# Differential attention: two query tiles' scores in one run of matmuls, and projections with two PSUM banks

## The chip, the cores and the metric

The kernel runs on one NeuronCore of a Trainium2 chip. Its metric is the device time of one execution in microseconds. The core's engines work side by side, each through its own list of instructions: TensorE (PE) multiplies into PSUM, which has eight banks of 512 fp32 columns for 128 partitions; VectorE (DVE) and ScalarE (ACT) read the banks and do everything else that is elementwise; SyncE (SP) issues the loads.

## What is computed

Two layers over 256 latent and 256 context tokens of width 1024. A layer normalizes its input, feeds three mixers (a recurrent one, multi-head latent attention, differential attention), adds them through gates, and ends with a feed-forward part. The changed part is differential attention, with 8 heads, two maps of queries and keys of width 64, and one map of values of width 128:

```python
def _attention(q, k, v, mix_w, scale):
    # out = sum_m mix_w[m] * softmax(scale * q_m k_m^T) v
    def block(qi):
        s = jnp.einsum('bqmhd,bkmhd->bmhqk', qi, k).astype(jnp.float32) * scale
        p = jnp.einsum('m,bmhqk->bhqk', w, jax.nn.softmax(s, axis=-1))
        return jnp.einsum('bhqk,bkhd->bqhd', p.astype(v.dtype), v)
...
wc = jnp.stack([jnp.ones((), jnp.float32), -lam])
o_c = _attention(_diff_qk(dq, lp['diff_q_g'], rope_diff), jnp.concatenate([kd_l, kd_c], axis=1),
                 jnp.concatenate([vd_l, vd_c], axis=1), wc, DIFF_SCALE)
...
if need_ctx:      # layer 0 only: context queries read context keys alone
    o_cc = _attention(_diff_qk(dqc, lp['diff_q_g'], None), kd_c, vd_c, wc, DIFF_SCALE)
```

## The kernel before

Every fp32 operand is split into a high and a low part (names ending in H and L), and a product is three matmuls, high by high, low by high and high by low (L200 to L202). Weights are streamed in pieces of 128 x 1024 by SP and split on the way: ScalarE writes the high part (`wh`), VectorE the low part (`wl`; both L138). In layer 1 there are more weight buffers, whose tile is called `room`.

Tokens are worked in tiles of 128. Layer 0 has four query tiles (0 and 1 latent, 2 and 3 context) and layer 1 the two latent ones. Latent queries see 512 keys, context queries 256.

A scheduler places the instructions on the engines by a priority that counts up as the code is written. Work written as a generator stands in a queue, and `fill(ns)` draws from it so many nanoseconds of matmuls, so that projections fill PE between the steps of attention. `PAIR_FIRST` (2000) puts the score matmuls ahead. Each engine then runs its list in order, and a waiting instruction holds up all behind it.

PSUM's banks are given out by pools with tags, each tag in rotation: a tile gets its bank when the last reader of the tile before in that bank is done. Before the change `mm` (L93) has three banks for projections, `tr` two for transposes, and three more are given out anew by stage (`three_banks`, L100): in the stage of differential attention one pair of banks, tag `S2`, for the scores of both maps of one query tile, and one bank `sc` for the product with the values (`po`).

That stage, from 298 to 560 us in layer 0 and 1398 to 1580 us in layer 1, is the loop at L1133. For head i it writes: `diff_prep(i + 1)` (transposes `dtrk` and `dtrq`, split into `dkH`, `dkL`, `dqH`, `dqL`); `probs_T` of head i - 1 (transposes `ptr` of the probabilities, split into `pH` and `pL`); `diff_sc(i)` (scores `S` at L663, softmax with one maximum on VectorE, L621, and one exponential `dp` on ScalarE, L623, for each tile and map, then the difference of the maps, L966); `diff_sub(i - 2)` (`subt2`); and `diff_pv(i - 1)` (`po`, twelve matmuls, copied by ScalarE to `so`, L989, transposed to `subt`, normalized). `diff_proj` makes queries, keys and values of two heads through `gemm_tm` (L449), and `v_tm` splits the values from the projection's bank into `dvH` and `dvL`, tiles of a pool with six buffers (`t_v`). `gemm_tm` loads each of the two halves of a weight once and works it through all token tiles, so that four token tiles hold two banks, `pst0` and `pst1`, from the first half to the second.

At the stage's end, beside the last heads, the queue holds the first projections of the recurrent branch and of the gates: `rnn_conv` (L1021), a convolution of four taps, one operation on ScalarE (L1030) and three on VectorE (L1034) for each projection's bank, which layer 0 first copies out of PSUM to `xr` (L1025) and layer 1 reads in place; and `branch_gate` (L1114), whose bank ScalarE copies to `gt` (L1118).

## Time and profile before

| | us |
|---|---|
| median of three runs (1972.23, 1972.54, 1977.07) | 1972.54 |
| profiled execution | 1974.12 |
| its span | 1972.3 |
| TensorE busy | 1930.2 |
| VectorE busy | 1568.3 |
| ScalarE busy | 1069.9 |

The span runs from the first to the last instruction of the core. Busy time of an engine is the time in which it has an instruction in work; matmuls overlap, so that their durations add up to more than the time they take. In a timeline the difference of two starts is what a matmul costs. The granted clock is the share of TensorE's full speed: 1.0 is 2.4 GHz and 0.5 is 1.2 GHz.

### The profile page before, as it was taken

Reading aid. Unit: us, or ns where it says so; the run is one execution under the profiler, and the core shown is the slowest. Engines: PE = TensorE matmul, PEld = TensorE weight load, DVE = VectorE, ACT = ScalarE, POOL = GpSimd, SP = SyncE. Lnnn points to the kernel's source line nnn. Section 1 sums busy time; section 2 is a strip of 40 time slices with the busy share of each in tenths; the row PEclk is TensorE's granted clock in tenths of the full one; section 3 lists DMA queues with packets and bytes.
Section 4 is the critical chain, followed back from the end, with each engine's and each line's share of the span. In section 5 each row is a group of like instructions: output and inputs, shape, how many; then the busy total and the mean of one; then the engine's idle time right before and its main releaser. Section 6 shows DMA issues by size and latency. Waiting matters only on the chain. (4 is left out here: it accounts for less than half of the span.)

```text
span 1972.3 us, 31832 instructions
## 1 busy us (share of the span) xinstructions
PE 1930.2 (98%) x11746; PEld 1666.3 (84%) x11746; DVE 1568.3 (80%) x3838; ACT 1069.9 (54%) x1975; POOL 58.8 (3%) x198
## 2 busy tenths in 40 slices
PE   7999999999999999999999999999999999899999
PEld 4888888988678878888888888988999788898888
DVE  5679965788798888789888876898688889966763
ACT  4568833455576663353233224798444678845552
POOL 0001000000000000000000000012010000000000
PEclk9999999999999999999999999999999999999999
DMA  8311122212234456536656653422322234474553
GB/s 291 99 41 51 53 65 77 76 55 67 70 102 129 140 191 197 184 127 201 196 191 201 200 176 115 151 64 76 128 93 80 65 123 143 156 231 150 185 189 108
DMA packets 91068, 258.16 MB, mean 131 GB/s; under 512 B 10144, under 2 KB 17312, under 8 KB 90656
## 3 DMA queue, kind: packets, MB, share of 16 engines
q1 hardware_dynamic: 90912, 256.13, 39.8%
q8 instruction: 92, 1.51, 0.3%
q14 instruction: 64, 0.52, 0.1%
HBM read 250.85 MB, written 5.24 MB: 130 GB/s over the span
## 5 line engine op out<-in xcount | busy, mean ns | idle before, releaser
L138 ACT ACTIVATE wh<-st 128x1024 fp32r<-128x1024 f32 (+4 forms) x305 | 308.4, 1012 | 367.8 <-PE ps L201 173.1
L138 DVE TENSOR_TENSOR wl<-st,wh 128x1024 fp32r<-128x1024 f32 (+4 forms) x305 | 354.2, 1162 | 125.5 <-ACT wh L138 122.0
L200 PE MATMUL ps<-hH,wh 128*128 128x512 f32 (+1 forms) x504 | 182.0, 361 | 3.8 <-ACT gt L1118 2.9
L202 PE MATMUL ps<-hH,wl 128*128 128x512 f32 (+1 forms) x504 | 180.6, 359 | 1.7 <-DVE wl L138 1.7
L201 PE MATMUL ps<-hL,wh 128*128 128x512 f32 (+1 forms) x504 | 181.3, 360 | 0.0
L200 PE MATMUL pst<-wh,hH 128*128 128x256 f32 x568 | 164.3, 289 | 0.0
L201 PE MATMUL pst<-wl,hH 128*128 128x256 f32 x568 | 162.1, 285 | 0.0
L202 PE MATMUL pst<-wh,hL 128*128 128x256 f32 x568 | 161.9, 285 | 0.0
L200 PE MATMUL ps<-h2H,wh 128*128 128x512 f32 (+1 forms) x368 | 139.1, 381 | 0.7 <-ACT h2H L379 0.7
L201 PE MATMUL ps<-h2L,wh 128*128 128x512 f32 (+1 forms) x368 | 139.5, 380 | 0.0
L202 PE MATMUL ps<-h2H,wl 128*128 128x512 f32 (+1 forms) x368 | 139.5, 380 | 0.0
L621 DVE TENSOR_REDUCE st<-S 128x1 f32<-128x512 f32 (+1 forms) x192 | 113.0, 596 | 21.4 <-ACT dp L623 11.2
L138 DVE TENSOR_TENSOR room<-acc,room 128x1024 fp32r<-128x1024 f32 (+3 forms) x75 | 87.6, 1169 | 30.6 <-ACT room L138 29.1
L200 PEld LDWEIGHTS pst<-wh,hH 128*128 128x128 f32 x568 | 108.6, 191 | 3.8 <-issue 3.3
L200 PEld LDWEIGHTS ps<-hH,wh 128*128 128x128 f32 x504 | 95.3, 189 | 19.3 <-ACT gt L1118 3.9
L202 PEld LDWEIGHTS pst<-wh,hL 128*128 128x128 f32 x568 | 108.5, 191 | 1.7 <-issue 1.4
L201 PEld LDWEIGHTS pst<-wl,hH 128*128 128x128 f32 x568 | 108.6, 191 | 1.1 <-issue 0.7
L202 PEld LDWEIGHTS ps<-hH,wl 128*128 128x128 f32 x504 | 95.2, 189 | 15.6 <-DVE wl L138 2.3
L310 DVE SCALAR_TENSOR_TENSOR ms<-ms,cb 128x512 f32<-128x512 f32 x160 | 107.3, 688 | 1.3
L138 ACT ACTIVATE room<-acc 128x1024 fp32r<-128x1024 f32 (+3 forms) x75 | 76.2, 1017 | 57.6 <-PE ps L201 20.5
L201 PEld LDWEIGHTS ps<-hL,wh 128*128 128x128 f32 x504 | 95.3, 189 | 12.8
L310 DVE SCALAR_TENSOR_TENSOR sq<-ms,cb 128x512 f32<-128x512 f32 x112 | 75.7, 689 | 31.9 <-DMA ms<-wmodt 31.0
(585 smaller groups left out, 5558.3 us busy)
## 6 DMA issues: line engine op xcount, KB each, us to landing
st<-wfm SPq DMA_DIRECT2D x224, 512.0 KB, 3.5
ms<-wmodt SPq DMA_DIRECT2D x160, 256.0 KB, 2.8
acc<-wfm SPq DMA_DIRECT2D x56, 512.0 KB, 3.5
st<-wfo SPq DMA_DIRECT2D x35, 512.0 KB, 3.5
mstage<-wmod SPq DMA_DIRECT2D x16, 512.0 KB, 5.3
acc<-wfo SPq DMA_DIRECT2D x9, 512.0 KB, 3.5
st<-wlru SPq DMA_DIRECT2D x7, 512.0 KB, 3.4
st<-wukv SPq DMA_DIRECT2D x13, 256.0 KB, 2.6
```

The lines of the kernel that those rows point to most:

```text
L138: return A.activation(dH, src, AF.Copy), V.tensor_tensor(out=dL, in0=src, in1=f(dH), op=ALU.subtract)
L200: nc.tensor.matmul(ps, wH, xH, start=start, stop=False, skip_group_check=skip)
L201: nc.tensor.matmul(ps, wH, xL, start=False, stop=False, skip_group_check=skip)
L202: nc.tensor.matmul(ps, wL, xH, start=False, stop=stop, skip_group_check=skip)
L310: issue_after(V.scalar_tensor_tensor(out=o, in0=st, scalar=1.0, in1=cb[:, v, :], op0=ALU.mult, op1=ALU.mult, accum_out=sums[:, i - i0, h, ...
L621: V.tensor_reduce(out=st[:, 0:1], in_=S, axis=AX.X, op=ALU.max, negate=True)
```

## The change

The three banks of a stage become four, and `mm` keeps two fixed ones. Outside the stage of differential attention the fourth is the third `mm` bank, as before. Inside it the four are two pairs `S2`: projections have two banks, and `po` takes a bank of a pair.

`scores2` now takes two query tiles. For the latent tiles it takes both pairs, one for a tile; for the context tiles, which have 256 keys, one pair, each tile in one half of the columns. The twelve matmuls (two tiles, three products, two maps) are chained one behind the other, where there were two runs of six. The first waits for the last readers of the tiles that were in its banks (`readers`, in which each exponential and each copy of `po` is entered). In layer 1 the run takes its tiles in reverse.

`gemm_tm` works one pair of token tiles through both halves of the weight before the next, so that one bank at a time is filled, and keeps both halves until the end.

```diff
-    def ps_mm(name):
-        return pp.tile([P, 512], F32, tag="mm", name=name, bufs=3)
...
+    def four_banks(stage, two):
 
         if spare[0] is not None:
             spare[0].close()
         spare[0] = ctx.enter_context(ExitStack())
         banks[0] = spare[0].enter_context(tc.tile_pool(name=stage, bufs=1, space=PSUM, reuse_waits="tile"))
-
-    three_banks("sc")
-    singles = [3]
+        pairs[0] = two
+
+    four_banks("sc", False)
+    third = [0]
+
+    def ps_mm(name):
+        third[0] = (third[0] + 1) % 3
+        if third[0] == 0 and not pairs[0]:
+            return banks[0].tile([P, 512], F32, tag="mm", name=name, bufs=1)
+        return pp.tile([P, 512], F32, tag="mm", name=name, bufs=2)
+
+    readers, taken = {}, [0]
+
+    def ps_pair(name):
+        taken[0] += 1
+        return banks[0].tile([P, 2, 512], F32, tag="S2", name=name, bufs=2)
 
     def ps_sc(name):
-        return banks[0].tile([P, 512], F32, tag="sc", name=name, bufs=singles[0])
+        if pairs[0]:
+            return ps_pair(name)[:, 0, :]
+        return banks[0].tile([P, 512], F32, tag="sc", name=name, bufs=3)
...
     def gemm_tm(l, widx, xH, xL, toks, ps_, consume):
 
-        pss = [ps_(f"pst{i}").rearrange("p (t n) -> p t n", t=2) for i in range(len(toks) // 2)]
-        for hf in range(2):
-            H, L = wload(wfm[l, widx, hf])
-            H = H.rearrange("p (k n) -> p k n", n=256)
-            L = L.rearrange("p (k n) -> p k n", n=256)
-            for i, tt in enumerate(toks):
-                for kk in range(4):
-                    k = hf * 4 + kk
-                    mm3(pss[i // 2][:, i % 2, :], xH[:, k, tt * P:(tt + 1) * P], xL[:, k, tt * P:(tt + 1) * P], H[:, kk, :], L[:, kk, :], k == 0 and i % 2 == 0, k == KT - 1 and i % 2 == 1, True)
-                if hf == 1 and i % 2 == 1:
-                    consume(toks[i - 1], pss[i // 2])
-                yield 12 * mm_ns(256)
+        W = []
+        for t0 in toks[::2]:
+            ps = ps_("pst").rearrange("p (t n) -> p t n", t=2)
+            for hf in range(2):
+                if t0 == toks[0]:
+                    W.append([w_.rearrange("p (k n) -> p k n", n=256) for w_ in wload(wfm[l, widx, hf])])
+                H, L = W[hf]
+                for i in range(2):
+                    tok = slice((t0 + i) * P, (t0 + i + 1) * P)
+                    for kk in range(4):
+                        k = hf * 4 + kk
+                        mm3(ps[:, i, :], xH[:, k, tok], xL[:, k, tok], H[:, kk, :], L[:, kk, :], k == 0 and i == 0, k == KT - 1 and i == 1, True)
+                    if hf == 1 and i == 1:
+                        consume(t0, ps)
+                    yield 12 * mm_ns(256)
...
-            def scores2(qH, qL, kH, kL, tt):
-
-                k0 = 0 if tt < 2 else SEQ
+            def scores2(qH, qL, kH, kL, tts):
+
+                ctx_ = tts[0] >= 2
+                k0 = SEQ if ctx_ else 0
                 n = T - k0
-                both = banks[0].tile([P, 2, 512], F32, tag="S2", name="S", bufs=1)
-                S = [both[:, m, :] for m in range(2)]
-                tok = slice(tt * P, (tt + 1) * P)
+                both = [ps_pair("S") for _ in range(1 if ctx_ else 2)]
+                at_ = {tt: taken[0] if ctx_ else taken[0] - 1 + i for i, tt in enumerate(tts)}
+                S = {tt: [both[0][:, m, i * n:(i + 1) * n] if ctx_ else both[i][:, m, :] for m in range(2)] for i, tt in enumerate(tts)}
                 before = None
-                for i, (q_, k_) in enumerate(((qH, kH), (qH, kL), (qL, kH))):
-                    for m in range(2):
-                        K = slice(64 * m, 64 * m + 64)
-                        mm = nc.tensor.matmul(S[m][:, :n], q_[K, tok], k_[K, k0:], start=(i == 0), stop=(i == 2), tile_position=(64 * m, 0))
-                        if before is not None:
-                            issue_after(mm, before)
-                        else:
-                            tc.cur_priority -= PAIR_FIRST
-                        before = mm
+                for at, tt in enumerate(tts[::-1] if last else tts):
+                    tok = slice(tt * P, (tt + 1) * P)
+                    for i, (q_, k_) in enumerate(((qH, kH), (qH, kL), (qL, kH))):
+                        for m in range(2):
+                            K = slice(64 * m, 64 * m + 64)
+                            mm = nc.tensor.matmul(S[tt][m], q_[K, tok], k_[K, k0:], start=(i == 0 and not (ctx_ and at)), stop=(i == 2 and not (ctx_ and at == 0)), tile_position=(64 * m, 0), skip_group_check=ctx_)
+                            if before is not None:
+                                issue_after(mm, before)
+                            else:
+                                for b_ in set(at_.values()):
+                                    if b_ - 2 in readers:
+                                        issue_after(mm, readers[b_ - 2])
+                                tc.cur_priority -= PAIR_FIRST
+                            before = mm
                 tc.cur_priority += PAIR_FIRST
-                return [s_[:, :n] for s_ in S]
+                return S, at_
...
                 for tt in qtoks:
+                    if tt % 2 == 0:
+                        S, at_ = scores2(*qk, (tt, tt + 1))
                     p1 = pc[0][1] if tt == 3 else t_p("dp1")
                     sl = slice(0, 512) if tt < 2 else slice((tt - 2) * 256, (tt - 1) * 256)
                     p2 = t_p("dp2")
                     rr = []
-                    S = scores2(*qk, tt)
                     for m, dst, total in ((0, p1[:, sl], s0[:, tt:tt + 1]), (1, p2[:, sl], None)):
-                        rr.append(softmax_raw(S[m], rq[:, tt, 2 * hh + m:2 * hh + m + 1], dst, total))
+                        rr.append(softmax_raw(S[tt][m], rq[:, tt, 2 * hh + m:2 * hh + m + 1], dst, total))
+                    readers[at_[tt]] = last_exp[0]
                     V.scalar_tensor_tensor(out=rr[1], in0=rr[1], scalar=s0[:, tt:tt + 1], in1=nlam, op0=ALU.mult, op1=ALU.mult)
...
             def diff_pv(h):
                 o = ps_sc("po")
+                at_ = taken[0]
...
-                A.activation(u[:, :TQ], o[:, :TQ], AF.Copy)
+                readers[at_] = A.activation(u[:, :TQ], o[:, :TQ], AF.Copy)
...
-            three_banks(f"pair{l}")
-            singles[0] = 1
+            four_banks(f"pair{l}", True)
+            readers.clear()
...
-            three_banks(f"single{l}")
-            singles[0] = 3
+            four_banks(f"single{l}", False)
```

In the changed kernel the lines of the three matmuls of a product are L212 to L214, that of the scores is L681.

PE at the first scores of head 1 in layer 0 (`S` are scores, `pst` a projection, `dtrk` and `dtrq` transposed keys and queries; x2 stands for the two maps), before:

```order
L201 MATMUL pst1_4515<-wl_4519,hH_145 128x256
L202 MATMUL pst1_4515<-wh_4518,hL_146 128x256
L663 MATMUL S_4606<-dkH_3864,dqH_3873 128x512 x2
L663 MATMUL S_4606<-dkL_3865,dqH_3873 128x512 x2
L663 MATMUL S_4606<-dkH_3864,dqL_3874 128x512 x2
L200 MATMUL pst1_4515<-wh_4518,hH_145 128x256
L201 MATMUL pst1_4515<-wl_4519,hH_145 128x256
```

and in the changed kernel:

```order
L214 MATMUL pst_4513<-wh_4546,hL_146 128x256
L681 MATMUL S_4608<-dkH_3864,dqH_3873 128x512 x2
L681 MATMUL S_4608<-dkL_3865,dqH_3873 128x512 x2
L681 MATMUL S_4608<-dkH_3864,dqL_3874 128x512 x2
L681 MATMUL S_4609<-dkH_3864,dqH_3873 128x512 x2
L681 MATMUL S_4609<-dkL_3865,dqH_3873 128x512 x2
L681 MATMUL S_4609<-dkH_3864,dqL_3874 128x512 x2
L960 MATMUL dtrk_4562<-ident_92,ddk_4421 128x128
L960 MATMUL dtrk_4562<-ident_92,ddk_4427 128x128
```

Where one query tile's run of six stood between projection matmuls, one run has the six of both tiles.

PE behind the product with the values (`po`) of head 0 in layer 0, up to its transposes `subt`; the last `po` matmul stands five rows ahead of the first row here, before:

```order
L201 MATMUL pst0_4868<-wl_4873,hH_145 128x256
L202 MATMUL pst0_4868<-wh_4872,hL_146 128x256
L663 MATMUL S_4704<-dkH_3864,dqH_3873 128x256 x2
L663 MATMUL S_4704<-dkL_3865,dqH_3873 128x256 x2
L663 MATMUL S_4704<-dkH_3864,dqL_3874 128x256 x2
L200 MATMUL pst0_4868<-wh_4872,hH_145 128x256
L201 MATMUL pst0_4868<-wl_4873,hH_145 128x256
L202 MATMUL pst0_4868<-wh_4872,hL_146 128x256
L992 MATMUL subt_4772<-ident_92,so_4770 128x128 x4
L939 MATMUL dtrk_4800<-ident_92,ddk_4447 128x128
```

and in the changed kernel, from the last two `po` matmuls on:

```order
L1010 MATMUL po_4755<-pL_4604,dvH_3905 128x256
L1011 MATMUL po_4755<-pH_4603,dvL_3906 128x256
L1016 MATMUL subt_4770<-ident_92,so_4768 128x128 x4
L960 MATMUL dtrk_4798<-ident_92,ddk_4421 128x128
L960 MATMUL dtrk_4798<-ident_92,ddk_4427 128x128
L960 MATMUL dtrk_4798<-ident_92,ddk_4485 128x128
L960 MATMUL dtrk_4798<-ident_92,ddk_4487 128x128
L212 MATMUL pst_4873<-wh_4876,hH_145 128x256
L213 MATMUL pst_4873<-wl_4877,hH_145 128x256
```

Before, matmuls of the next projection and a run of scores stand between `po` and `subt`; now `subt` follows at once, and the next projection (`pst_4873`) comes behind it.

PE near the end of the stage in layer 1, where the second bank of the convolution's projection ends (`ps1`) and the gate's projection begins (`ps0_17715` before, `ps0_17707` now), before:

```order
L201 MATMUL ps1_17516<-hL_12521,room_12752 128x512
L202 MATMUL ps1_17516<-hH_12520,room_12752 128x512
L200 MATMUL ps0_17715<-hH_12520,wh_17718 128x256
L986 MATMUL po_17569<-pL_17491,dvH_17116 128x256
L987 MATMUL po_17569<-pH_17490,dvL_17117 128x256
L985 MATMUL po_17569<-pH_17490,dvH_17116 128x256
L986 MATMUL po_17569<-pL_17491,dvH_17116 128x256
L987 MATMUL po_17569<-pH_17490,dvL_17117 128x256
L201 MATMUL ps0_17715<-hL_12521,wh_17718 128x256
L202 MATMUL ps0_17715<-hH_12520,wl_17719 128x256
```

and in the changed kernel:

```order
L213 MATMUL ps1_17515<-hL_12513,room_12744 128x512
L214 MATMUL ps1_17515<-hH_12512,room_12744 128x512
L1016 MATMUL subt_17576<-ident_92,so_17574 128x128 x2
L650 MATMUL ptr_17645<-ident_92,dp1_17501 128x128
L650 MATMUL ptr_17645<-ident_92,dp1_17531 128x128
L650 MATMUL ptr_17645<-ident_92,dp1_17501 128x128
L650 MATMUL ptr_17645<-ident_92,dp1_17531 128x128
L1009 MATMUL po_17668<-pH_17650,dvH_17110 128x256
L212 MATMUL ps0_17707<-hH_12512,wh_17710 128x256
L213 MATMUL ps0_17707<-hL_12513,wh_17710 128x256
```

The gate's projection stood right behind the last matmul of `ps1`, in a third bank; now the rest of the attention stands between, and its bank is that of `ps0_17514`, the convolution's other projection.

VectorE in the changed kernel at that place (`room` is a weight's low part, `dp1` the difference of the maps, `subr` and `subrt` small steps of the normalization, `xc` the convolution out of the banks `ps0` and `ps1`):

```order
L150 TENSOR_TENSOR room_12744<-acc_12745,room_12744 128x1024
L640 RECIPROCAL st4_17537<-st4_17537 128x1
L224 SCALAR_TENSOR_TENSOR subrv_17584<-subss_17580,s0_17383 128x2
L988 SCALAR_TENSOR_TENSOR st4_17537<-st4_17537,s0_17486,nlam_10259 128x1
L225 TENSOR_SCALAR subr_17586<-subrv_17584 128x2
L989 SCALAR_TENSOR_TENSOR dp1_17531<-dp2_17532,st4_17537,dp1_17531 128x512
L226 TENSOR_SCALAR subr_17586<-subr_17586 128x2
L1058 SCALAR_TENSOR_TENSOR xc_17615<-ps0_17514,prm1_83,xc_17615 128x2x254
L229 SCALAR_TENSOR_TENSOR subrt_17585<-subr_17586 128x2
L1058 SCALAR_TENSOR_TENSOR xc_17636<-ps1_17515,prm1_83,xc_17636 128x2x254
L230 TENSOR_TENSOR subrt_17585<-subrt_17585,subrv_17584 128x2
L1058 SCALAR_TENSOR_TENSOR xc_17615<-ps0_17514,prm1_83,xc_17615 128x2x255
```

The operations of the two convolutions stand in turns, with the small steps between them; three more follow.

## Rows read from the trace of the kernel before

**Rows 1.** The page, busy time of each engine (share of the span), instructions.

```profile
PE 1930.2 (98%) x11746; PEld 1666.3 (84%) x11746; DVE 1568.3 (80%) x3838; ACT 1069.9 (54%) x1975; POOL 58.8 (3%) x198
```

**Rows 2.** Waits of PE by line: total us, times, longest us.

```profile
PE ps L202 <- DVE room L138: 5.5, 2, 4.1
PE ps L200 <- ACT gt L1118: 2.9, 2, 2.2
...
PE S L663 <- ACT dp L623: 0.6, 2, 0.3
```

**Rows 3.** Timeline of PE around one run of scores: start us, duration us, operation.

```profile
452.59 0.28 PE L202 MATMUL pst<-wh,hL 128*128 128x256 f32 x1
452.80 0.39 PE L663 MATMUL S<-dkH,dqH 64*128 64x256 f32 x2
453.02 0.28 PE L663 MATMUL S<-dkL,dqH 64*128 64x256 f32 x2
453.14 0.28 PE L663 MATMUL S<-dkH,dqL 64*128 64x256 f32 x2
453.35 0.39 PE L200 MATMUL pst<-wh,hH 128*128 128x256 f32 x1
453.57 0.28 PE L201 MATMUL pst<-wl,hH 128*128 128x256 f32 x1
```

**Rows 4.** Instructions on tile S: count, ns min/median/max, first and last start, forms.

```profile
L663 PE MATMUL S<-dkH,dqH x96: 381/493/503, 298.5 to 1564.8; 64*128 64x512 f32 x64, 64*128 64x256 f32 x32
```

**Rows 5.** Timeline of PE in layer 1's tail, with [idle before <- releaser].

```profile
1557.98 0.50 PE L663 MATMUL S<-dkH,dqH 64*128 64x512 f32 x2 [0.30 <-ACT dp L623]
...
1559.38 0.98 PE L635 MATMUL ptr<-ident,dp 128*128 128x128 f32 x7 [0.43 <-DVE dp L966]
...
1566.48 0.30 PE L635 MATMUL ptr<-ident,dp 128*128 128x128 f32 x1 [0.34 <-DVE dp L966]
```

**Rows 6.** Timeline of PE from the last po matmul to subt, layer 0.

```profile
465.58 0.28 PE L987 MATMUL po<-pH,dvL 128*128 128x256 f32 x1
...
466.55 0.66 PE L992 MATMUL subt<-ident,so 128*128 128x128 f32 x4
```

**Rows 7.** Groups of ScalarE by line and form, 290 to 560 us: busy, mean ns | idle.

```profile
L138 ACT ACTIVATE wh<-st 128x1024 fp32r<-128x1024 f32 x33 | 34.9, 1057 | 35.6 <-PE ps L201 24.1 <-PE pst L202 11.3
L623 ACT ACTIVATE dp<-S,st,drq 128x512 f32<-128x512 f32 x32 | 24.9, 777 | 17.0 <-DVE st L622 15.5 <-DVE subrt L218 1.5
...
L138 ACT ACTIVATE pH<-ptr 128x512 fp32r<-128x512 f32 x24 | 14.1, 597 | 12.1 <-PE ptr L638 7.5 <-PE ptr L635 4.6
...
L138 ACT ACTIVATE dvH<-pst 128x256 fp32r<-128x256 f32 x16 | 5.9, 380 | 9.2 <-PE pst L202 4.9 <-DVE dvL L138 2.5 <-PE po L986 1.8
...
L989 ACT ACTIVATE so<-po 128x512 f32<-128x512 f32 x8 | 4.8, 597 | 1.7 <-PE po L987 1.7
```

**Rows 8.** Timeline of VectorE in layer 1's tail.

```profile
1563.99 1.23 DVE L138 TENSOR_TENSOR room<-acc,room 128x1024 fp32r<-128x1024 f32 x1 [0.89 <-ACT room L138]
...
1565.58 0.75 DVE L966 SCALAR_TENSOR_TENSOR dp<-dp,st,dp 128x512 f32<-128x512 f32 x1
1566.25 0.74 DVE L1034 SCALAR_TENSOR_TENSOR xc<-ps,prm,xc 128x508 f32<-128x508 f32 x1
...
1568.30 0.16 DVE L213 TENSOR_SCALAR subr<-subrv 128x2 int32<-128x2 int32 x1
1568.37 0.74 DVE L1034 SCALAR_TENSOR_TENSOR xc<-ps,prm,xc 128x510 f32<-128x510 f32 x1
```

**Rows 9.** Timeline of PE after a wait of layer 1, 1717 to 1720 us.

```profile
1716.89 0.58 PE L202 MATMUL ps<-hH,room 128*128 128x256 f32 x1 [4.14 <-DVE room L138]
...
1719.84 0.32 PE L200 MATMUL ps<-hH,room 128*128 128x256 f32 x1
1719.99 0.28 PE L201 MATMUL ps<-hL,room 128*128 128x256 f32 x1
```

**Rows 10.** One stretch: length, busy us (count) by engine, PEclk, DMA share, GB/s.

```profile
1717.00:1720.00 3.00, 3.00 (x15) 3.00 (x16) 3.00 (x8) 0.11 (x1) 0.00 (x0) 0.51 0.67 196
```

More of the change, by code (lines that the diff above doesn't have):

```diff
@@ L90, in tile_hybrid @@
     pp = ctx.enter_context(tc.tile_pool(name="pp", bufs=1, space=PSUM, reuse_waits="tile"))
-    def ps_mm(name):
-        return pp.tile([P, 512], F32, tag="mm", name=name, bufs=3)
     def ps_tr(name):
         return pp.tile([P, 512], F32, tag="tr", name=name, bufs=2)
-    spare, banks = [None], [None]
-    def three_banks(stage):
+    spare, banks, pairs = [None], [None], [False]
+    def four_banks(stage, two):
         if spare[0] is not None:
@@ L287, in first_mod @@
         V.tensor_scalar(out=am[:, :, t], in0=modt[0][:, 1, :, t], scalar1=1.0, scalar2=prmt[0][:, N1 + t:N1 + t + 1], op0=ALU.add, op1=ALU.mult)
-    first_sq, last_h, last_out = [None], [None], [None]
+    first_sq, last_h, last_out, last_exp = [None], [None], [None], [None]
     def mod_vectors(wk, t_sq, soon, later):
@@ L622, in softmax_raw @@
                 V.tensor_tensor(out=st[:, 1:2], in0=st[:, 0:1], in1=sc_ap, op=ALU.mult)
-                A.activation(dst, S, AF.Exp, scale=sc_ap, bias=st[:, 1:2], accum_out=st[:, 2:3] if total is None else total)
+                last_exp[0] = A.activation(dst, S, AF.Exp, scale=sc_ap, bias=st[:, 1:2], accum_out=st[:, 2:3] if total is None else total)
                 if total is None:
```

## The prediction

> **What bounds the kernel now.** I read the busy shares first, then what TensorE waits for, then single stretches of its timeline. TensorE (PE) is busy for 1930.2 of the 1972.3 us span, 98% [rows 1]; VectorE has 1568.3 us and ScalarE 1069.9 us in the same span. So only what shortens PE's own sequence, or what makes PE wait, moves the end. The list of PE's waits [rows 2] is short: 5.5 us in two waits for the low part of a streamed weight (`room`), 2.9 us in two waits for the gate's copy (`gt`, L1118), and for a free pair of score banks (`S` L663, on the exponentials `dp`) only 0.6 us in all. Busy time is a poor price list here, because matmuls are pipelined: a 256-column matmul has a duration of 0.28 us but the next one starts 0.12 us later (453.02 to 453.14) [rows 3]. All prices of PE below are therefore differences of starts.
>
> **The sum is made** against the profiled execution (span 1972.3, 1974.12 us with what lies around it). The median of the three runs is 1972.54 us, 1.6 us less; I apply the same difference to the median. A measurement of this kernel can tell some 0.3%, 5.9 us, from no change: faster is below 1966.6, slower above 1978.4.
>
> **Term A, fewer runs of two-map matmuls.** The score matmuls use 64 rows of the array each and go two at a time. Around one run of six the steps are [rows 3]: 0.21 into the run (452.59 to 452.80), 0.22 for its first pair, 0.12 for the second, 0.21 out of it and 0.22 for the first 128-row matmul behind it. The steady step is 0.12, so a run pays 0.09 + 0.10 + 0.09 + 0.10 = 0.38 us for going in and coming out, independent of its length. There are 288 two-map instructions (96 of each of three forms; one of them in [rows 4]), the same before and after. In the written order they stand in 51 runs before and 27 after (48 tiles of scores in sixes against 24 pairs of tiles in twelves; the first of each layer is split up in both). 24 runs less at 0.38 is **-9.1 us**. All of it lies on PE, which is the bound, so nothing hides it. Bounds: if the second tile's first pair, which has new weights and a new bank, pays its 0.10 again, 24 x 0.28 = -6.7; the upper end is the 0.38 itself. I take the upper end, since inside a run the weights change at every pair and the third of them shows no excess.
>
> **Term B, waits that go.** The two `gt` waits (2.9) [rows 2] stand in layer 0's tail, where a projection takes the bank of a gate's projection just ended, which ScalarE has not yet copied. In the new order a dozen 512-column matmuls into the other bank stand between: **-2.9**. In layer 1's tail PE now waits for exponentials and probabilities between single tiles (0.30 + 0.43 + 0.34) [rows 5]; with two tiles in one run the next transposes come later than their input: **-1.0**. What is late next in both tails is D and E.
>
> **Term C, heads 0, 2 and 4 of layer 0.** Projections have two banks instead of three. Before, behind the last `po` matmul of a head six projection matmuls start before `subt` does: 465.58 to 466.55 is 0.97 us, of which 7 x 0.12 is work and 0.13 lost [rows 6]. Now `subt` stands directly (or one matmul) behind `po`, as the order above shows, because the next projection has no bank: the values of the heads ahead are evicted from it into `t_v`, whose six buffers still hold what this `po` reads. On ScalarE two `dvH` copies (which wait for `po`) stand ahead of the `so` copy, on which `subt` waits. Queued behind the waiting `subt` on PE are all projections. The price: two `dvH` at 0.28 between starts (duration 0.38), one `so` of 0.60 [rows 7], less the 0.13 already lost, about 1.05 each: **+3.1** for three. Bounds: 0.5 each if the copies start before `po` ends (1.5), 1.6 each if VectorE's `dvL` is late too (4.8).
>
> **Term D, layer 0's tail, head 7.** The run for its two context tiles needs the pair of banks of its first tile. Between PE's transposes and that run ScalarE has one `pH`, one `wh`, another `pH` and the second exponential: 0.60 + 1.06 + 0.60 + 0.78 = 3.0 by durations [rows 7]; PE has 4 matmuls of 512 columns and 8 transposes between, about 1.4 us. **+1.7**. Bounds 1.0 (the exponential goes ahead) and 3.5 (the whole chain behind it, the reduction of VectorE too).
>
> **Term E, layer 1's tail.** In layer 1 the convolution reads its projection's bank directly, with one ScalarE and three VectorE operations. Before, the gate's first projection took the free third bank and began right behind the last projection matmul. Now it needs the bank of `ps0`, and VectorE works the two convolutions off in turns, so five of the six operations come first. The chain from the last matmul of `ps1` on, which also frees the weight buffer `room`: ScalarE's split of `room`, 1.06 (`wh`, same shape) [rows 7]; VectorE's part of it, 1.15 of its 1.23; `dp`, 0.67 from 1565.58 to the next start at 1566.25; five convolution operations at 0.66 (0.74 long); some nine small operations at 0.07 (1568.30 to 1568.37) to 0.16, about 0.9 in all [rows 8]: 7.1 us. PE has two `subt2`, four `ptr` and one `po` meanwhile, 0.9. **+6.2**. The trace has no wait of this kind, so its ends are far apart: 2 us, if VectorE has done `room` and the convolutions of the first half when `ps1` ends, and 9 us, if the reductions that this trace has in the same stretch also come first. I take the worked-out value, because VectorE has no gap in the stretch that I read but the 0.89 us ahead of `room` [rows 8].
>
> **Clock.** The nearest row to such a wait is the one for `room` near 1717 us, 4.14 us long. Behind it 13 steps take 2.95 us (1716.89 to 1719.84) [rows 9] instead of 13 x 0.12 = 1.56, with a granted clock of 0.51, the lower of the two levels (1.2 GHz) [rows 10]. The same behind E costs **+1.4**; between 0 (the waits for `gt`, shorter, show in the same list) and 2.8.
>
> **Nothing else.** The order of PE outside the two attention stages changes at a few places by single fills; POOL, the DMA queue of SP and all counts stay as they are. `gemm_tm` holds both weight halves longer, but no weight comes late for it in [rows 2]. I cost these at 0.
>
> **Sum:** -9.1 - 2.9 - 1.0 + 3.1 + 1.7 + 6.2 + 1.4 = **-0.6**, 1971.9 us.
>
> **Rivals.** (1) *The new waits are small.* C 1.5, D 1.0, E 2.0 and no lower clock: -13.0 + 4.5 = -8.5, 1964.0 us. For it: VectorE is busy 80% on average and PE's list of waits is short, so the engines keep up well today. Against it: the two tails are just where the list has its waits. (2) *Evacuation becomes the bound at the tails, slower.* With two projection banks PE stops whenever ScalarE and VectorE are behind: E 9.0, clock 2.8, D 3.5, C 4.8 make +20.1, less 13.0 is +7.1, 1979.6 us. It decides from 18.9 us of new waits on (13.0 + 5.9). For it: VectorE is without a gap at E's place; against it: only 0.6 us of waiting for score banks in the whole trace [rows 2]. The Trainium skill, "TensorEngine Tiling (Array Packing)", section "PSUM Bottleneck", says that tiling makes TensorE faster but not the emptying of PSUM, which may then become the bottleneck; by that rule this rival would be the likeliest one, and the trace agrees with it at the `gt` waits (2.9 us) but not at the score banks (0.6 us). (3) *A run of twelve saves only part*: each second tile pays its entry again, -6.7 in place of -9.1, and PE also waits in the middle of some runs for the second pair of banks: about 1974.3 us. That the change would not do what it says is ruled out by the order, which has the twelves.
>
> **How the numbers follow.** Forecast 1971.9 with 0.46, its own range 1967 to 1977; rival 1 0.27; rival 2 0.17; rival 3 0.10. Faster takes rival 1's 0.27, slower rival 2's 0.17, the same 0.56. The range reaches from 1962.5, a little below rival 1, to 1979.7, rival 2's worked-out value; it leaves out about 0.1 on each side.
>
> **What would show it.** Steps around the runs of twelve: 0.38 in excess and none between the sixth and the seventh pair (A). In PE's list of waits: no `gt` (B); `subt` on `so` in three places of about 1 us (C); `S` L681 on `dp` about 1.7 (D); `ps` on `xc`, L1058, about 6 us, and a granted clock near 0.5 behind it (E). The prediction is wrong if E is missing (then rival 1), or if other waits for projection banks appear inside the stages, where I costed none (then rival 2).

## The result, and the profile after

The changed kernel takes 1986.43 us (median of four runs, 1984.57 to 1988.71), the kernel before 1973.98 (four runs beside it): a ratio of 1.0062, 95% interval 1.0049 to 1.0074, so 12 us slower. The profiled execution has a span of 1984.4 us against 1972.3. The page of the changed kernel, busy time by engine:

```profile
PE 1925.9 (97%) x11746; PEld 1671.1 (84%) x11746; DVE 1567.2 (79%) x3838; ACT 1069.6 (54%) x1975; POOL 57.0 (3%) x198
```

Against [rows 1] no engine has more instructions, and PE is busy for slightly less time in a longer span: what was added is mostly waiting. PE's waits by line in the changed kernel (total us, times, longest us), those of the attention stage:

```profile
PE ps L214 <- DVE room L150: 5.5, 2, 4.2
PE dtrq L965 <- DVE dkL L150: 3.3, 4, 0.9
PE ptr L650 <- DVE dp L989: 3.1, 2, 2.8
PE ptr L650 <- DVE so L1024: 2.7, 4, 1.2
...
PE ptr L650 <- DVE dqL L150: 2.2, 2, 1.1
...
PE po L1009 <- ACT dp L638: 1.9, 1, 1.9
PE ps L212 <- DVE xc L1058: 1.8, 1, 1.8
...
PE subt L1016 <- ACT so L1013: 1.5, 1, 1.5
PE pst L212 <- DVE dvL L150: 1.5, 1, 1.5
PE ps L212 <- DVE dvL L150: 1.5, 1, 1.5
```

The first row is the old wait of [rows 2], unchanged; the waits for `gt` are gone, all others are new or grown. Added up over the tiles of the attention stage (`dtrk`, `dtrq`, `ptr`, `subt`, `S`, `po`, and projections that wait for `gt`, `dvL` or `xc`), the list has 7.7 us before and 24.3 us after, 16.6 us more. Two stretches at half clock (below) add some 4 us, and 24 runs fewer take 9.1 off: 16.6 + 4.1 - 9.1 = 11.6, against 12.1 between the two profiled spans.

PE around one run of twelve in the changed kernel:

```profile
373.64 0.28 PE L214 MATMUL pst<-wh,hL 128*128 128x256 f32 x1
373.85 0.39 PE L681 MATMUL S<-dkH,dqH 64*128 64x256 f32 x2
374.07 0.28 PE L681 MATMUL S<-dkL,dqH 64*128 64x256 f32 x2
374.19 0.28 PE L681 MATMUL S<-dkH,dqL 64*128 64x256 f32 x2
374.31 0.28 PE L681 MATMUL S<-dkH,dqH 64*128 64x256 f32 x2
...
374.54 0.28 PE L681 MATMUL S<-dkH,dqL 64*128 64x256 f32 x2
374.75 0.39 PE L212 MATMUL pst<-wh,hH 128*128 128x256 f32 x1
374.98 0.28 PE L213 MATMUL pst<-wl,hH 128*128 128x256 f32 x1
```

The steps are those of [rows 3]: 0.21 in, 0.22 for the first pair, 0.21 out, 0.23 behind it, and 0.12 at each pair between, at the seat between the tiles too (374.19 to 374.31). The run of twelve pays its entry once, as term A has it.

VectorE at a place inside layer 0's stage, and below it PE at the same time:

```profile
422.39 0.69 DVE L636 TENSOR_REDUCE st<-S 128x1 f32<-128x512 f32 x1 [1.00 <-ACT dp L638]
423.00 0.68 DVE L150 TENSOR_TENSOR dqL<-dtrq,dqH 128x512 fp32r<-128x512 f32 x1
```

```profile
423.74 0.44 PE L650 MATMUL ptr<-ident,dp 128*128 128x128 f32 x2 [1.11 <-DVE dqL L150]
```

VectorE stands still for 1.00 us, because the maximum of the second map waits for the exponential of the first; the split `dqL`, which would give the bank of `dtrq` back, is queued behind it, and `ptr` on PE waits 1.11 us for that bank. This wait of VectorE is not new (11.2 us in all before, 10.1 after, by the group of L621 or L636); what is new is that PE waits behind it.

PE at layer 0's tail (term D) and the granted clock of that stretch (length, busy us and count by engine, PEclk, DMA share, GB/s):

```profile
516.02 0.44 PE L650 MATMUL ptr<-ident,dp 128*128 128x128 f32 x2 [0.81 <-DVE so L1024]
...
517.21 0.66 PE L650 MATMUL ptr<-ident,dp 128*128 128x128 f32 x4 [0.54 <-DVE pL L150]
518.49 0.39 PE L681 MATMUL S<-dkH,dqH 64*128 64x256 f32 x2 [0.62 <-ACT dp L638]
518.71 0.33 PE L681 MATMUL S<-dkL,dqH 64*128 64x256 f32 x2
518.84 0.41 PE L681 MATMUL S<-dkH,dqL 64*128 64x256 f32 x2
519.05 0.42 PE L681 MATMUL S<-dkH,dqH 64*128 64x256 f32 x2
...
522.84 0.79 PE L1009 MATMUL po<-pH,dvH 128*128 128x512 f32 x1 [1.90 <-ACT dp L638]
523.43 0.63 PE L1010 MATMUL po<-pL,dvH 128*128 128x512 f32 x1
...
528.98 0.44 PE L214 MATMUL ps<-hH,wl 128*128 128x512 f32 x1
```

```profile
518.00:529.00 11.00, 8.61 (x31) 6.64 (x32) 10.04 (x26) 6.55 (x16) 0.00 (x0) 0.54 0.15 49
```

The clock falls to its lower level, 1.2 GHz, inside the run: its steps grow from 0.13 us (518.71 to 518.84) to 0.21 (518.84 to 519.05). That is ahead of the wait of 1.90, and it lasts until 529 us (0.54 in this stretch, which begins before the fall). Behind the wait 13 steps take 5.55 us (523.43 to 528.98) instead of 13 x 0.23, which costs 2.6 us. And at layer 1's tail (term E):

```profile
1572.89 0.55 PE L650 MATMUL ptr<-ident,dp 128*128 128x128 f32 x3 [2.79 <-DVE dp L989]
1574.12 0.58 PE L1009 MATMUL po<-pH,dvH 128*128 128x256 f32 x1 [0.69 <-ACT pH L150]
1576.52 0.58 PE L212 MATMUL ps<-hH,wh 128*128 128x256 f32 x1 [1.81 <-DVE xc L1058]
1576.89 0.41 PE L213 MATMUL ps<-hL,wh 128*128 128x256 f32 x1
...
1580.31 0.31 PE L214 MATMUL ps<-hH,wl 128*128 128x256 f32 x1
```

Three waits, 5.3 us by the list (6.2 from start to start), and behind them 16 steps (1576.89 to 1580.31) in 3.42 us instead of 16 x 0.12: the same lower level, 1.5 us.

### The profile page after: what moved, and what is told of

The parts are those of the page before. It is cut to its first block, busy times and chain, and to the rows that moved or that the text cites. A ratio compares the mean times of both kernels' runs of the same rounds, so it can differ in the third digit from the quotient of the medians.

```text
span 1984.4 us, 31834 instructions
## 1 busy us (share of the span) xinstructions
PE 1925.9 (97%) x11746; PEld 1671.1 (84%) x11746; DVE 1567.2 (79%) x3838; ACT 1069.6 (54%) x1975; POOL 57.0 (3%) x198
## 4 chain that ended last, share of the span: by engine, by line
PE 77%; DVE 13%; ACT 6%; issue 2%; DMA 2%; SPq 0%; DVEq 0%; ACTq 0%
PE ps L212 11%; PE ps L214 11%; PE ps L213 11%; PE ps L440 4%; PE pst L212 3%; PE pst L214 3%; PE pst L213 3%; PE po L214 2%; PE po L213 2%; PE po L212 2%; PE ptr L650 2%; PE po L850 2%; PE ps L441 2%; DVE wl L150 2%; DMA ms<-wmodt 1%
## 5 line engine op out<-in xcount | busy, mean ns | idle before, releaser
L212 PE MATMUL ps<-hH,wh 128*128 128x512 f32 (+1 forms) x504 | 183.8, 365 | 4.5 <-DVE xc L1058 1.8
L214 PE MATMUL ps<-hH,wl 128*128 128x512 f32 (+1 forms) x504 | 181.8, 362 | 1.8 <-DVE wl L150 1.6
L212 PE MATMUL pst<-wh,hH 128*128 128x256 f32 x568 | 163.1, 287 | 1.5 <-DVE dvL L150 1.5
L214 PE MATMUL pst<-wh,hL 128*128 128x256 f32 x568 | 161.9, 285 | 0.0
L212 PE MATMUL ps<-h2H,wh 128*128 128x512 f32 (+1 forms) x368 | 139.1, 381 | 0.6 <-ACT h2H L391 0.6
L214 PE MATMUL ps<-h2H,wl 128*128 128x512 f32 (+1 forms) x368 | 139.5, 380 | 0.0
L636 DVE TENSOR_REDUCE st<-S 128x1 f32<-128x512 f32 (+1 forms) x192 | 112.4, 595 | 21.8 <-ACT dp L638 10.1
L212 PEld LDWEIGHTS ps<-hH,wh 128*128 128x128 f32 x504 | 96.6, 192 | 19.5 <-ACT wh L150 2.3
L212 PEld LDWEIGHTS pst<-wh,hH 128*128 128x128 f32 x568 | 108.7, 191 | 3.3 <-DVE dvL L150 1.7
L214 PEld LDWEIGHTS ps<-hH,wl 128*128 128x128 f32 x504 | 96.7, 192 | 16.2 <-DVE wl L150 2.6
L214 PEld LDWEIGHTS pst<-wh,hL 128*128 128x128 f32 x568 | 108.7, 191 | 1.1 <-issue 1.0
```

The lines of the kernel that those rows point to most:

```text
L212: nc.tensor.matmul(ps, wH, xH, start=start, stop=False, skip_group_check=skip)
L214: nc.tensor.matmul(ps, wL, xH, start=False, stop=stop, skip_group_check=skip)
L636: V.tensor_reduce(out=st[:, 0:1], in_=S, axis=AX.X, op=ALU.max, negate=True)
```

## The experiments

Two theories were set against each other. Theory A: the run of twelve hands VectorE four banks of scores at once, and its second reductions wait for exponentials, so the transposes' banks come back late. Theory B: with two projection banks, filled one at a time, PE has nothing to do when a transpose waits. Each kernel stands beside runs of the kernel before on the same chip (median 1973.9 to 1974.7 us). Differences between experiments are taken from the ratios times 1974.

**The changed banks with runs of six.**

```diff
-                    if tt % 2 == 0:
-                        S, at_ = scores2(*qk, (tt, tt + 1))
+                    S, at_ = scores2(*qk, (tt,))
...
-                both = [ps_pair("S") for _ in range(1 if ctx_ else 2)]
+                both = [ps_pair("S")]
```

> The changed kernel with its banks and its gemm_tm, but the score matmuls in runs of six again, each query tile (the context tiles too) in a pair of banks of its own, two pairs in rotation. Theory A (burst): the run of twelve gives VectorE four banks of scores at once, and each second reduction waits for the first exponential with the splits of the transposes queued behind it; so with runs of six PE's waits for the transposes' banks (ptr, dtrq, dtrk on VectorE, some 13 us in the changed kernel) fall to about 4 us, the 24 entries of runs come back (+9 us), and the time stays near 1986 us. Theory B (banks): two projection banks, filled one at a time, leave PE without other work when a transpose waits; the length of the run has no part in it. Then these waits stay, the entries come on top, and the time is about 1995 us.

Measured: 1988.64 us, ratio 1.0074 (1.0059 to 1.0089), +14.6 us. The transposes' waits fell by 5 us only (14.2 to 8.8), and others came in their place (`po` on `dp` 3.7, `S` on `dp` 2.2). So the runs of twelve bring 2.4 us in this layout (the two intervals overlap), not 9.1, and the banks with `gemm_tm` alone cost as much as the whole change loses. VectorE's second reductions wait only 2.5 us for exponentials here, where they waited 10.1 us in the changed kernel:

```profile
DVE st L636 <- ACT dp L638: 2.5, 4, 1.0
```

The loss is there without most of that wait. Theory A by its number of 4 us falls, theory B by its 1995 us.

**The changed kernel with a tile for each map.**

```diff
-        return banks[0].tile([P, 2, 512], F32, tag="S2", name=name, bufs=2)
+        return [banks[0].tile([P, 512], F32, tag=f"S{m}", name=name, bufs=2) for m in range(2)]
```

> The changed kernel, but the scores of the two maps lie in two tiles of one bank each instead of one tile of two banks; runs, banks and all else as in the changed kernel. The reduction of the second map then waits for PE and no longer for the exponential of the first. Theory A (burst, and VectorE held up by that wait with the splits queued behind it): waits of ptr and dtrq on VectorE fall by 6 to 9 us, 1977 to 1980 us. Theory B (banks): they stay, 1985 to 1987 us.

Measured: 1974.83 us, ratio 1.0004 (0.9995 to 1.0014): 11.4 us less than the changed kernel, more than theory A asked for, though the waits of `ptr` and `dtrq` fell by 4.4 us alone (13.6 to 9.2) and not by its 6 to 9. The second reduction of a latent tile no longer waits for ScalarE. At the place shown above VectorE now reads:

```profile
422.30 1.28 DVE L636 TENSOR_REDUCE st<-S 128x1 f32<-128x512 f32 x2
...
423.56 0.68 DVE L636 TENSOR_REDUCE st<-S 128x1 f32<-128x512 f32 x1
...
424.23 0.68 DVE L636 TENSOR_REDUCE st<-S 128x1 f32<-128x512 f32 x1
...
425.07 0.69 DVE L150 TENSOR_TENSOR dqL<-dtrq,dqH 128x512 fp32r<-128x512 f32 x1
```

VectorE has no gap, but the four reductions of one run stand ahead of `dqL`: this is the burst. Its waits, and that of a run's second tile for the bank that `po` took, are what is left on PE:

```profile
PE dtrq L965 <- DVE dkL L150: 5.6, 6, 1.0
...
PE S L681 <- ACT so L1013: 4.4, 3, 1.6
```

Most of the gain came from elsewhere: the tails (`po`, `xc`, `so`) and their half clock. The edit has a second effect: `po` now lies in a bank that only the first map's exponential reads, so it need not wait for the second's.

**The kernel before with a tile for each map.**

```diff
-                both = banks[0].tile([P, 2, 512], F32, tag="S2", name="S", bufs=1)
-                S = [both[:, m, :] for m in range(2)]
+                S = [banks[0].tile([P, 512], F32, tag=f"S{m}", name="S", bufs=1) for m in range(2)]
```

> The kernel before, with the scores of the two maps in two tiles of one bank each; all else as before. VectorE's idle time ahead of the second reduction goes. Theory A: PE waited little for it in the kernel before, so 0 to -3 us, 1970 to 1973 us. Theory B has no say in it: 1973 us.

Measured: 1983.53 us, ratio 1.0047 (1.0030 to 1.0063), a miss of both. PE's waits fell from 7.7 to 2.3 us, yet the kernel lost 9 us. PE in it shows why:

```profile
432.19 0.28 PE L200 MATMUL pst<-wh,hH 128*128 128x256 f32 x1
432.40 0.38 PE L662 MATMUL S<-dkH,dqH 64*128 64x256 f32 x1
432.71 0.38 PE L201 MATMUL pst<-wl,hH 128*128 128x256 f32 x1
432.93 0.28 PE L202 MATMUL pst<-wh,hL 128*128 128x256 f32 x1
...
433.50 0.38 PE L662 MATMUL S<-dkH,dqH 64*128 64x256 f32 x1
```

The first map's bank comes free before the second's, so its first matmul is placed alone, with projection matmuls behind it, and the other five follow later: 88 runs instead of 51. 37 x 0.38 = 14 us, less 5.4 of waits, is what it lost. This is the price of an entry (term A) a second time, from the other side. (The list is that of the attention stage, as above.)

**The kernel before with the context tiles in one run.** One pair of banks, each tile in half of the columns; latent tiles in sixes; three projection banks and `gemm_tm` as before.

```diff
-                    S = scores2(*qk, tt)
+                    if tt != 3:
+                        S = scores2(*qk, (tt,) if tt < 2 else (2, 3))
```

> The kernel before, with its three projection banks and its gemm_tm, but the two context tiles of a head in layer 0 scored in one run of twelve into one pair of banks, each tile in one half of the columns. Eight runs fewer at 0.38 us are -3.0 us. Theory A: the burst of four reductions, here of 256 columns, costs part of it again: 1970 to 1974 us. Theory B: three banks cover it, the full gain: 1970 us.

Measured: 1971.00 us, ratio 0.9986 (0.9977 to 0.9996), -2.8 us. Where no bank is given up, a run saved is a gain: 43 runs instead of 51, 8 x 0.38 = 3.0.

**`gemm_tm` alone,** in the kernel before: its loops over halves and token tiles exchanged, as in the diff of the change.

```diff
-        for hf in range(2):
...
-            for i, tt in enumerate(toks):
+        for t0 in toks[::2]:
+            ps = ps_("pst").rearrange("p (t n) -> p t n", t=2)
+            for hf in range(2):
```

> The kernel before, with three projection banks and runs of six, but with the changed gemm_tm, which fills one projection bank at a time. If the new waits come from the banks' number (theory B), this costs nothing: 1972 to 1975 us. If they come from gemm_tm, whose projection of two token tiles ends twice as often and asks for a bank each time (rival), PE's waits for the transposes' and the projections' banks appear here already, some 5 us or more: 1979 us or above.

Measured: 1976.10 us, ratio 1.0009 (0.9999 to 1.0019). +1.8 us, hardly to be told from nothing: it isn't the cause.

**The changed kernel with the `gemm_tm` of before,** the same lines the other way round:

```diff
-        for t0 in toks[::2]:
-            ps = ps_("pst").rearrange("p (t n) -> p t n", t=2)
+        pss = [ps_(f"pst{i}").rearrange("p (t n) -> p t n", t=2) for i in range(len(toks) // 2)]
+        for hf in range(2):
```

> The changed kernel with the gemm_tm of before, which holds two projection banks from the first half of a weight to the second, so both of the two that there are. Theory B (too few projection banks): no projection can start until the one before is copied out, so waits grow, 1987 to 1995 us. Rival (gemm_tm): the waits of the changed kernel for dvL and so (5 us) go, 1978 to 1982 us.

Measured: 1983.60 us, ratio 1.0047 (1.0032 to 1.0062), 3 us less than the changed kernel. `po` and `dvL` waits are as long as ever; `dtrq` and `ptr` wait 11 us instead of 13.6. Neither expectation holds: with two banks, taking both at once is no worse.

**The tile for each map, second map first.** To the kernel before with a tile for each map, the run begins with the bank that is free last:

```diff
-                    for m in range(2):
+                    for m in (1, 0):
```

> As the kernel before with the two maps' scores in two tiles, but each run begins with the second map, whose bank comes free last. In the run with two tiles and the first map first, 51 runs became 88, which costs 37 x 0.38 = 14 us, while PE's waits fell from 11.5 to 4 us. If that splitting was the whole loss, the runs are 51 again, the waits stay at 4 us and the time is 1965 to 1968 us. If the two tiles themselves cost something else, it stays above 1973 us.

Measured: 1969.29 us, ratio 0.9977 (0.9966 to 0.9988), -4.5 us. The runs are 51 again and PE's waits 3.5 us. The splitting was the loss: against the kernel with the first map first this is 13.8 us, and 37 runs at 0.38 are 14. The time is 1.3 us above the range that was expected.

**Both, on the banks of before:** context tiles in one run, a tile for each map, second map first.

```diff
-                both = banks[0].tile([P, 2, 512], F32, tag="S2", name="S", bufs=1)
-                S = [both[:, m, :] for m in range(2)]
+                both = [banks[0].tile([P, 512], F32, tag=f"S{m}", name="S", bufs=1) for m in range(2)]
+                S = {tt: [both[m][:, i * n:(i + 1) * n] for m in range(2)] for i, tt in enumerate(tts)}
...
-                    for m in range(2):
+                        for m in (1, 0):
```

> As the kernel before, with both: the context tiles' scores in one run of twelve in one pair of banks (measured -2.9 us alone) and the two maps in two tiles, second map first. 43 runs. If the two add up: 1962 to 1966 us. If the waits that the two tiles take away were needed as cover by the longer run, 1968 to 1971 us.

Measured: 1966.07 us (1965.64 to 1966.53), ratio 0.9956 (0.9941 to 0.9970): 8.7 us faster than the kernel before and 21 us faster than the changed one. The two parts (2.8 and 4.5) add up within their intervals.

**Two projection banks, nothing given for the third.** Runs of six and the changed `gemm_tm`; one pair for the scores, one bank for `po`, the eighth bank unused.

```diff
-        return banks[0].tile([P, 2, 512], F32, tag="S2", name=name, bufs=2)
+        return banks[0].tile([P, 2, 512], F32, tag="S2", name=name, bufs=1)
...
-            return ps_pair(name)[:, 0, :]
+            return banks[0].tile([P, 512], F32, tag="sc", name=name, bufs=1)
```

> The banks of the kernel before in the attention stage (one pair for scores, a bank of its own for po) and its runs of six, with the changed gemm_tm, but only two projection banks; the eighth bank is left unused there. Against the run with the changed gemm_tm and three banks (1976 us) this takes away one projection bank and nothing else. Theory B (the third projection bank is what the change lost): 1984 to 1990 us, as the run of six with two pairs in rotation (1988.6). Rival (po in a pair and the rotation of the pairs cost it): 1975 to 1979 us.

Measured: 2000.70 us, ratio 1.0129 (1.0114 to 1.0144). The missing bank costs 23.7 us against the run with three, more than theory B said, and the second pair of banks gives 11 of it back (1988.6). PE's largest wait here, and stretches of both layers' tails:

```profile
PE S L681 <- ACT dp L638: 10.9, 8, 3.9
```

```profile
514.70:528.20 13.50, 8.24 (x30) 5.33 (x31) 8.43 (x24) 5.45 (x14) 0.00 (x0) 0.50 0.13 39
535.20:538.50 3.30, 3.30 (x12) 2.59 (x13) 3.11 (x7) 1.33 (x3) 0.00 (x0) 0.50 0.02 5
1586.50:1593.20 6.70, 5.26 (x23) 5.00 (x24) 6.00 (x20) 2.25 (x5) 0.00 (x0) 0.50 0.00 0
```

By the list PE waits 25.1 us in the attention stage, 16.4 more than in the kernel with three banks and this `gemm_tm` (8.7). And 16.8 us of PE's work (8.24 + 3.30 + 5.26) lie at half clock, none there with three banks; an estimate of what that costs is half of it, 8 us. So up to a third of the 23.7 us is the clock's.

**The convolution copied out of PSUM in layer 1:**

```diff
-                if not last:
-                    xr = t_p("xr")
-                    A.activation(xr, ps, AF.Copy)
+                xr = t_p("xr")
+                A.activation(xr, ps, AF.Copy)
```

> The changed kernel, but the convolution of layer 1 first copies its projection out of PSUM with ScalarE, as layer 0 does, and so gives its bank back after one operation. If the bank that the convolution holds is what PE waits for in layer 1's tail (term E), the waits there (6.2 us) fall to about 3 and the stretch at half clock (1.5 us) goes: 1981 to 1983 us. If PE waits there for VectorE's probabilities anyway, only the last wait of 2.3 us goes: 1984 to 1985 us.

Measured: 1982.55 us, ratio 1.0041 (1.0026 to 1.0056), 4 us less than the changed kernel. The three waits of layer 1's tail (5.3 us by the list) are one of 2.2 us, and no stretch there is at half clock. Term E's mechanism stands. But the 4 us are not its price: the waits of the whole execution add up to as much as in the changed kernel (53.3 against 53.1 us), because what is won here is waited for later (`room`, `x`) and in layer 0's tail. What is shorter in the trace is the time at half clock, in layer 0's tail too, where the edit changes nothing: there 3.3 us of PE's work are at half clock instead of 8.3.

**The copy of `po` ahead of `dvH`:**

```diff
+                tc.cur_priority -= 2000
                 readers[at_] = A.activation(u[:, :TQ], o[:, :TQ], AF.Copy)
+                tc.cur_priority += 2000
```

> The changed kernel, with the copy of po (so) given a higher priority, so that it stands ahead of one or both of the dvH copies on ScalarE. If term C is what its working says (subt waits for so behind two dvH), the three waits behind po (5.1 us) shrink by 0.28 to 0.56 each: 1984.5 to 1985.5 us. If the projection's bank (dvL) is the later one, nothing changes: 1986.4 us.

Measured: 1985.66 us, ratio 1.0056 (1.0039 to 1.0073). The waits behind `po` shrank from 4.5 to 3.8 us by the list; the medians differ by 0.8 us, which these intervals can't tell from nothing. The direction fits term C, no more.

**Runs of six, a tile for each map, on the changed banks:** the first experiment's edit, with

```diff
-        return banks[0].tile([P, 2, 512], F32, tag="S2", name=name, bufs=2)
+        return [banks[0].tile([P, 512], F32, tag=f"S{m}", name=name, bufs=2) for m in range(2)]
...
-                        for m in range(2):
+                        for m in (1, 0):
```

> The changed kernel's banks and gemm_tm, runs of six, and the two maps' scores in two tiles, second map first. Against the same with runs of twelve (e2, 1974.8 us) only the run's length differs. If runs of twelve bring what the entries cost (24 x 0.38): 1983 to 1984 us. If the burst of four score banks costs that back: 1975 to 1978 us.

Measured: 1972.75 us, ratio 0.9988 (0.9978 to 0.9997), against 1.0004 with runs of twelve. With VectorE's gap gone, runs of twelve are no gain at all here, 2 to 3 us of loss. Their 21 runs fewer (29 against 50) are worth 8 us; the waits on PE are 17.7 us instead of 9.5. The run's length is not all that differs: this kernel begins with the second map, the one with runs of twelve with the first, which splits two of its runs (29 where the changed kernel has 27), 0.8 us at 0.38 each.

Against the kernel before with the same edit of the maps (1969.29 us, -4.5) this one is 2.1 us slower, and `gemm_tm` alone was 1.8. So with a tile for each map the changed banks cost next to nothing; with a tile of two banks they cost 12.8 us (14.6 less 1.8).

## Why the prediction was wrong

It forecast 1971.9 us, range to 1979.7; 1986.4 was measured. Nearest is rival 2: PE stops where the engines that empty PSUM are behind. But rival 2 put all of its price on the tails and on heads 0, 2 and 4; the waits that made the difference it did not name.

- **Term A** (-9.1) was right in its size per run: 0.38 for a run of twelve, none at its seat. What the sum left out is that a run of twelve also has a price behind it. In the changed banks it brings 2.4 us by run, and with a tile for each map nothing.
- **"Nothing else"** (0) is the step that failed. I costed waits only where the order moved work at the stages' ends and behind `po`. Inside the stages, the transposes `dtrq`, `dtrk` and `ptr` wait for their two banks: 14.2 us by the list, 2.8 of them at the last tail (E), against 2.5 before (3.3, less 0.8 that term B has already), so +8.9. I read VectorE's share of 80% as slack, and didn't look at its waits: the group of L621 had 11.2 us of idle time ahead of it, waiting for exponentials. That a third projection bank covered such gaps before is argued from the order of PE; the runs show only that the banks are what costs.
- **Term B** (-3.9): the `gt` waits are gone, as said, and so are the three short ones of layer 1's tail; E stands in their place.
- **Term C** (+3.1): the three places are right. Each costs 1.7 us from start to start, 5.1 less the 0.4 of before is +4.7, at the upper bound (4.8). An exponential stands ahead of the two `dvH` as well, and at two of the three places the bank (`dvL`) is the later one, the case of that bound.
- **Term D** (+1.7): the run waits 0.86 us from start to start, less than said. But `po` also takes a pair in rotation, that of the second latent tile, and waits 2.3 us for its last exponential; that wait was not in the sum, nor the half clock, which fell before it and costs 2.6 us behind it: +5.8 in all.
- **Term E and its clock** (+7.6): 6.2 and 1.5 us measured, 7.7. The size was right, and so was the chain on VectorE; but PE meets it in three steps, of which the first is the transposes' wait for `dp`, and only the last the convolution's bank. The fall of the clock was forecast with it; the cases at the end of this document show that such a wait can be followed by either level, so that part of the size was partly luck.

With these sizes the sum is -9.1 - 3.9 + 8.9 + 4.7 + 5.8 + 7.7 = +14.1, against +12.1 between the spans; 0.8 of the difference is waits outside the attention stage that are shorter (28.8 us by the list, 29.6 before), the rest is open. What is shown by runs: `gemm_tm` costs little (+1.8), the banks cost 12.8 (the run of six against that), the runs of twelve bring 2.4, and a tile for each map takes 11.4 us (twelve) and 17 us (six) away, about what the banks cost.

Why it does is not shown. VectorE's wait ahead of the second reduction is only part of it: with runs of six it is 2.5 us, and the loss is as large. What falls there with a tile for each map is the wait of `po` for `dp` (3.7 to 0.3 us), those for `dvL` and `xc` (4.0 to none), of `S` for `dp` (2.2 to none) and of the transposes (8.8 to 5.4), and the half clock in layer 0's tail (6.8 us of PE's work to none). No run separates the second reduction from the bank that `po` takes, nor was it tried alone that the changed kernel's runs are also chained behind the readers of their banks (`readers`). Of the 2 to 3 us that twelve lose to six with a tile for each map, the four reductions in a row and the wait of the second tile for `so` are seen in the trace; how much each has of it was not tried.

The Trainium skill, "TensorEngine Tiling (Array Packing)", section "PSUM Bottleneck", says that packing makes TensorE faster and not the emptying of PSUM. I weighed it against the score banks, where PE had waited 0.6 us. The trace agrees with it in other banks than those of the packed matmuls: after the change PE still waits 0.6 us for the score banks, but 13.6 us at `dtrq` and `ptr`, the transposes.

## What to carry to other kernels

Before a bank is taken from a pool, look at what the engines that empty the banks wait for, and not only at their busy shares: VectorE was busy for 80%, and still the transposes' waits grew from 3.3 to 14.2 us. A tile that spans two banks ties its readers together; a tile for each bank, begun with the one that comes free last, was worth more (4.5 us) than the longer runs, and made the changed banks nearly free. And a run made longer is a gain where it costs no bank: the context tiles in one run, in the halves of one pair, gave 2.8 us, where eight runs at 0.38 are 3.0.

## What was not expected of the hardware

Entering and leaving a run of 64-row matmuls costs 0.38 us of PE whether it has six or twelve, and a run of a single matmul pays about the same: 0.44 us in the split runs (432.19 to 432.93 us, three steps, less 0.24 for two projection matmuls and 0.06 for half a pair). The Trainium skill, same page, section "Key Properties", says that a change of the tiling mode drains TensorE; the trace agrees, and gives the price.

Of the clock: the waits alone do not tell when it falls. In layer 0's tail of the changed kernel it fell at 518.8 us, behind waits of 0.81, 0.54 and 0.62 us. The kernel that copies the convolution out of PSUM has the same three waits there and keeps the full clock, through a longer wait as well, until 525 us:

```profile
519.32 0.38 PE L681 MATMUL S<-dkH,dqH 64*128 64x256 f32 x2 [0.62 <-ACT dp L638]
...
523.67 0.50 PE L1009 MATMUL po<-pH,dvH 128*128 128x512 f32 x1 [2.79 <-ACT dp L638]
```

```profile
519.00:525.00 6.00, 2.90 (x22) 2.30 (x23) 5.79 (x16) 4.42 (x11) 0.00 (x0) 1.00 0.30 87
```

In the kernel before, the wait of 2.17 us for `gt` ([rows 2]) is followed by the full clock; columns as above:

```profile
530.52 0.50 PE L200 MATMUL ps<-hH,wh 128*128 128x512 f32 x1 [2.17 <-ACT gt L1118]
```

```profile
530.00:534.00 4.00, 3.48 (x18) 2.61 (x19) 2.96 (x8) 2.64 (x5) 0.00 (x0) 1.00 0.69 207
```

In the kernel with the context tiles in one run a wait of the same length at the same place is followed by half of it:

```profile
528.31 0.79 PE L200 MATMUL ps<-hH,wh 128*128 128x512 f32 x1 [2.17 <-ACT gt L1121]
```

```profile
528.30:531.40 3.10, 3.09 (x7) 2.48 (x8) 1.93 (x6) 2.17 (x4) 0.00 (x0) 0.50 0.82 238
```

What the two have different for the clock was not tried. So some microseconds of a difference between two kernels can be the clock's, with the waits unchanged.
